# One batch of the samples' mLSTM states behind each tile of the output gate's projection

## The chip, the cores and the metric

The kernel runs on one core of a Trainium2 chip. Its time is the device time of one execution in microseconds (us); three runs of the kernel before gave 2279.9 to 2281.02, median 2280.3. One further execution was recorded by the hardware profiler: 2277.65 us, of which 2275.9 lie between its first and its last instruction.

## What is computed

One inference step of a hybrid decoder layer, for a prompt (1024 tokens) and for samples (8 batches of 4 tokens), with the same weights; the kernel holds both as 1056 columns. What matters here is the mixer: an S5 branch, an mLSTM branch with four heads of 256 by 256 state, and gates that are projections of the same normalized input. Cut to the parts that the change touches:

```
u, qk_raw, v, o, ig, fg, gate_s5, gate_m = split(h @ w_in)
y_s5 = gelu(S5(u)); y_s5 = y_s5 * sigmoid(y_s5 @ s5_w_glu)
hm, c_new, n_new, m_new = mlstm(q, k, v, log_i, log_f, c0, n0, m0)
hm = rmsnorm(hm) * g_mhead * sigmoid(o)
merged = sigmoid(gate_s5) * (y_s5 @ w_s5_up) + sigmoid(gate_m) * (hm @ w_m_up)
x = x + merged @ w_out
```

For the samples every batch and head has its own state c0 (256 by 256): the step reads it (q times c0 goes into the numerator), scales it by a decay, adds k times v, and writes it back. That is 8 batches of 4 states, 256 KB each, read and written once.

## The kernel before

The program is traced in Python (`run`, L1511) for five engines and their DMA queues. The context is opened with `schedule_with_timeline_sim=True` (L1577): at build time a planner with a simulated timeline puts the instructions of each queue in order. Of what it holds ready it takes what was traced earlier, so the order of the Python calls is a priority, not the order on the chip. After the build every queue runs strictly in its own order.

Around the change, `run` calls in this order (L1535 to L1543):

- `head_proj` and `head_scan` for heads 0 to 3: the prompt's mLSTM, in 8 chunks a head. The running state sits in a tile called mlA; its last value goes out by two stores on SP, L1222 (the matrix, 256 KB) and L1223 (one column of it, 1 KB).
- `samples()` is called before the last `head_scan`. It prepares the samples' operands and returns the function `states`.
- `states()` (L1293): first the new n (matmul L1303, DVE L1308, transposes L1311). Then `snum`, the PSUM tile of the samples' numerator, is opened by the matmul L1316, and the loop over 8 batches begins. A batch takes two tiles c from the pool "slots" (34 buffers, shared by nearly all large tiles); each is filled by two loads from SP (L1329, 256 KB each) and gets a small DVE copy (L1330). One DVE product (L1325) masks the batch's k. Then come the small matmuls of q with the states (L1334, into `snum`) and of k with v (L1340, PSUM tile skv), four DVE updates of c (L1342) and four stores from the ACT queue (L1343). After the loop `head_out` normalizes `snum` (DVE, ACT and POOL, L1146 to L1158), the transpose hT_smp and a DVE product (L1346) follow, and two stores on SP put the samples' columns into the scratch d_hm (L1349).
- `proj_tanh(..., "og")`: the output gate o, 8 tiles of 128 rows. A tile is one weight load on SP (wr_og, L100), its split into two halves, and 3 column chunks of 24 matmuls (mm_og, L109 to L111); a chunk leaves through DVE L614 and ACT L615 and is stored to the scratch d_to (L616).
- `s5_out_load` (L1357): four tiles yf of the S5 result come back from the scratch d_y (pool "r", two buffers), each goes through a gelu on ACT into y5f (L1365, L1366) and is split into y5h (ACT L92) and y5l (DVE L93).
- `s5_out` (L1372): the matmuls mm_glu on y5h and y5l, the small transposes cvT of `conv_out`, the matmuls mm_s5u, and `gated_heads`, which loads d_hm and d_to back.

The loads of `s5_out_load`, and those of L1390, L1405 and L1406, go through one helper. It ties the load behind the instruction that was traced just before it on the same engine, here SP; the planner may not put it ahead of that one:

```
    def pinned_load(self, dst, src):
        self.tc.keep_in_program_order(self.nc.sync.dma_start(dst, src))
...
    def s5_out_load(self):
...
        for mt in range(4):
            yf = self.pr.tile([P, RW], F32, tag="r", name=f"yf{mt}")[:, :1088].rearrange("p (t c) -> p t c", t=8)
            self.pinned_load(yf, self.d_y[mt * P:(mt + 1) * P])
```

Of the kernel before, what the change touches and what calls it, by code (L numbers as in the profile page):

```python
# [7 lines left out]
F32 = mybir.dt.float32  # L8
# [7 lines left out]
P = 128  # L16
# [5 lines left out]
XW = 1096  # L22
# [13 lines left out]
class Kernel:  # L36
# [562 lines left out]
            for s in range(8):  # L599
                nc.sync.dma_start(self.d_u[8 * mt:8 * mt + 8, s], ut[:, s])  # L600

    def proj_tanh(self, xn, rb, w, dst, name):

        nc = self.nc
        for m in range(KT):
            wt = self.weight(w[:, m * P:(m + 1) * P], f"{name}{m}")
            self.tanh_tile(xn, rb, wt, dst[m], f"{name}{m}")

    def tanh_tile(self, xn, rb, wt, dst, name):
        nc = self.nc  # L610
        for j, (o, n) in enumerate(CH):
            ps = self.unit(wt, xn, j, f"{name}_{j}")
            t = self.pt.tile([P, 384], F32, tag="sg", name=f"t_{name}_{j}")[:, :n]
            nc.vector.tensor_tensor(t, ps, rb[:, o:o + n], ALU.mult)  # L614
            nc.scalar.activation(t, t, AF.Tanh, scale=0.5)  # L615
            nc.scalar.dma_start(dst[:, o:o + n], t)  # L616
# [619 lines left out]
    def samples(self):  # L1236

        nc, v, a, pc = self.nc, self.nc.vector, self.a, self.pc
# [5 lines left out]
        x = self.px.tile([P, XW], F32, tag="s", name="smA")  # L1244
        rb, W, asb = x[:, 0:32], x[:, 32:64], x[:, 64:192].rearrange("p (h t) -> p h t", h=4)
# [23 lines left out]
        s = self.pv.tile([P, 512], F32, tag="aux", name="sS")[:, :32]  # L1269
# [23 lines left out]
        def states():  # L1293

            for h in range(4):
                v.tensor_copy(bm4[:, 8 * h:8 * h + 8], self.bmask)
            for h in range(4):
                for g in range(4):
                    if g != h:
                        v.memset(bm4[32 * g:32 * g + 32, 8 * h:8 * h + 8], 0.0)  # L1300
            ps = self.pv.tile([P, 512], F32, tag="aux", name="nn")[:, :64].rearrange("p (k h b) -> p k b h", k=2, h=4)
            for kk in range(2):
                nc.tensor.matmul(ps[:, kk].rearrange("p b h -> p h b"), kT[:, kk * P:(kk + 1) * P], bm4.rearrange("p (h b) -> p h b", h=4), start=True, stop=True)  # L1303
            dv = self.decb.rearrange("p (h c) -> p c h", h=4)[:, 8:16]
            for kk in range(2):
                n3 = nn[:, kk].rearrange("p (b h) -> p b h", h=4)
                v.tensor_tensor(n3, nz[:, :, kk, 0].rearrange("p (b h) -> p b h", h=4), dv, ALU.mult)
                v.tensor_tensor(n3, n3, ps[:, kk], ALU.add)  # L1308
            ps = self.pv.tile([P, 512], F32, tag="aux", name="nnT")[:32, :256]
            for kk in range(2):  # L1310
                nc.tensor.transpose(ps[:, kk * P:(kk + 1) * P], nn[:, kk], self.ident)  # L1311
            no = self.pt.tile([P, 384], F32, tag="h", name="no")[:32, :256]
            v.tensor_copy(no, ps)
            nc.sync.dma_start(self.outs[11][0].rearrange("b h k -> (b h) k"), no)
            num = self.pv.tile([P, 512], F32, tag="aux", name="snum")[:, :258]
            nc.tensor.matmul(num, Pb, self.vs, start=True, stop=False)  # L1316
            for b in range(8):
                bs = slice(4 * b, 4 * b + 4)
                qb = qm[b % 2]
                if b > 1:  # L1320
                    v.memset(qb[:, :, 4 * b - 8:4 * b - 4], 0.0)
                v.tensor_tensor(qb[:, :, bs].rearrange("p (h k) t -> p h k t", k=2), self.qs[:, :, bs].rearrange("p (h k) t -> p h k t", k=2),
                                asb[:, :, bs].unsqueeze(2).to_broadcast([P, 4, 2, 4]), ALU.mult)
                km = kms[b % 2]
                v.tensor_scalar(km, K[:96, :NP].bitcast(F32).rearrange("p (h x) -> p h x", h=4), self.bmask[:96, b:b + 1], None, op0=ALU.mult)  # L1325
                for hh in range(2):
                    ct = self.px.tile([P, XW], F32, tag="s", name=f"c0_{b}{hh}")[:, :1032].rearrange("p (h k x) -> p h k x", h=2, k=2)
                    for i in range(2):
                        nc.sync.dma_start(ct[:, i, :, 0:256], a["state_mlstm_c"][0, b, 2 * hh + i].rearrange("(k p) x -> p k x", p=P))  # L1329
                    v.tensor_copy(ct[:, :, :, 256:258], nz[:, 4 * b + 2 * hh:4 * b + 2 * hh + 2])  # L1330
                    for kk in range(2):
                        for i in range(2):
                            h = 2 * hh + i
                            nc.tensor.matmul(num[32 * h:32 * h + 32], qb[:, 2 * h + kk], ct[:, i, kk],  # L1334
                                             start=False, stop=b == 7 and kk == 1)
                    for i in range(2):
                        h = 2 * hh + i
                        kv = self.pv.tile([P, 512], F32, tag="aux", name=f"skv{b}_{h}").rearrange("p (k x) -> p k x", k=2)
                        for kk in range(2):
                            nc.tensor.matmul(kv[:, kk], km[:, h, kk * P:(kk + 1) * P], V[:96, 256 * h:256 * h + 256], start=True, stop=True)  # L1340
                        cc = ct[:, i, :, 0:256]
                        v.scalar_tensor_tensor(cc, cc, self.decb[:, 16 * h + 8 + b:16 * h + 9 + b], kv, op0=ALU.mult, op1=ALU.add)  # L1342
                        nc.scalar.dma_start(self.outs[10][0, b, h].rearrange("(k p) x -> p k x", p=P), cc)  # L1343
            ps, hT = self.head_out(num, em, P, "smp")()
            gm = self.gain["g_mhead"]
            v.tensor_tensor(hT.rearrange("p k (h t) -> p k h t", h=4), ps.rearrange("p k (h t) -> p k h t", h=4),  # L1346
                            gm.rearrange("p (h k) -> p k h", k=2).unsqueeze(3).to_broadcast([P, 2, 4, 32]), ALU.mult)
            for kk in range(2):
                nc.sync.dma_start(self.d_hm[kk::2, :, NP:NT].rearrange("h p t -> p h t"), hT[:, kk].rearrange("p (h t) -> p h t", h=4))  # L1349
# [161 lines left out]
    def run(self):  # L1511
        a, nc = self.a, self.nc
        w_in = a["w_in"][0]
        self.consts()
        self.d_xs = self.pd.tile([KT, P, NT], F32, name="d_xs")
        self.d_h = {q: self.pd.tile([16, P, NT], F32, name=f"d_{q}h") for q in ("f1", "f2")}
        F, st = self.first_pair(a["w1_gate"][0], a["w1_up"][0], "f1")
        xm, hook, sm = self.norm("g_mix", "n2")
        self.ffn(a["w1_gate"][0], a["w1_up"][0], a["w1_down"][0], F, st, "f1", hook, u0=1)
        self.scratch()  # L1520
        for m in range(KT):
            nc.sync.dma_start(self.d_x[m], self.x[m])
        self.dump("x1", self.x)
        rb = sm["rb"]
        self.mlstm_consts()
        self.s5_load()
        self.gates(xm, rb, w_in)
        self.proj_u(xm, rb, w_in)
        self.s5_prep()
        self.head_setup()  # L1530
        self.s5()
        self.proj_tanh(xm, rb, w_in[:, 4616:5640], self.d_t5, "gs")
        self.proj_tanh(xm, rb, w_in[:, 5640:6664], self.d_tm, "gm")
        self.scan_setup()
        for h in range(4):  # L1535
            qkv = self.head_proj(xm, sm, w_in, h)
            if h == 3:
                states = self.samples()
            self.head_scan(h, *qkv)
        states()  # L1540
        self.proj_tanh(xm, rb, w_in[:, 3584:4608], self.d_to, "og")
        self.s5_out_load()
        self.s5_out()  # L1543
        F, hook, st = self.norm_s("g_ffn2", "n3")
        self.join(hook)
        self.dump("x2", self.x)
        xp, hook, sp = self.norm("g_ple", "n4", "x")
        self.ffn(a["w2_gate"][0], a["w2_up"][0], a["w2_down"][0], F, st, "f2", hook, self.ple_in)
        self.dump("x3", self.x)
        self.ple(xp, sp, self.output())  # L1550
        self.dump("x4", self.x)
# [29 lines left out]
```

## Time and profile before

| | us |
|---|---|
| median of 3 runs (lowest, highest) | 2280.3 (2279.9, 2281.02) |
| the profiled execution, its own time | 2277.65 |
| its span, first to last instruction | 2275.9 |
| TensorE matmuls (PE) busy | 2234.4 (98%) |
| VectorE (DVE) busy | 1385.0 (61%) |
| ScalarE (ACT) busy | 823.4 (36%) |
| mean TensorE clock granted, as a share of full speed | 0.995 |

The profiled execution lies 2.65 us under the median of the runs. Durations below come from it alone. In the rows, PE is the matmul stream and PEld its weight loads; SPq, ACTq and DVEq stand for what a queue itself does (issuing a DMA, waiting), which does not count as busy. An idle time stands in square brackets with what ended it. Matmuls overlap their neighbours: a record of 0.34 us takes some 0.18 us of the stream, as the starts of the records show.

### The profile page before, as it was taken

Reading aid. Unit: us, or ns where it says so; the run is one execution under the profiler, and the core shown is the slowest. Engines: PE = TensorE matmul, PEld = TensorE weight load, DVE = VectorE, ACT = ScalarE, POOL = GpSimd, SP = SyncE. Lnnn points to the kernel's source line nnn. Section 1 sums busy time; section 2 is a strip of 40 time slices with the busy share of each in tenths; the row PEclk is TensorE's granted clock in tenths of the full one; section 3 lists DMA queues with packets and bytes.
Section 4 is the critical chain, followed back from the end, with each engine's and each line's share of the span. In section 5 each row is a group of like instructions: output and inputs, shape, how many; then the busy total and the mean of one; then the engine's idle time right before and its main releaser. Section 6 shows DMA issues by size and latency. Waiting matters only on the chain.

```text
span 2275.9 us, 39780 instructions
## 1 busy us (share of the span) xinstructions
PE 2234.4 (98%) x15711; PEld 2198.8 (97%) x15711; DVE 1385.0 (61%) x3189; ACT 823.4 (36%) x1560; POOL 514.8 (23%) x536
## 2 busy tenths in 40 slices
PE   7899999999999999999999999999999999999999
PEld 6899999999999999999999979999999999999998
DVE  5855556335868857678686477546655456523754
ACT  6433323113434433344444333224433233311543
POOL 1576664000000100000000000003476666100000
PEclk9999999999999999999999999999999999999999
DMA  6123226322454542112223587442222232711201
GB/s 198 59 76 94 71 61 232 123 72 69 125 125 125 142 127 67 52 48 69 64 58 97 162 277 249 136 149 83 64 71 81 75 95 86 269 64 54 61 20 77
DMA packets 288099, 240.47 MB, mean 106 GB/s; under 512 B 28652, under 2 KB 266188, under 8 KB 287912
## 3 DMA queue, kind: packets, MB, share of 16 engines
q1 hardware_dynamic: 268672, 216.34, 31.1%
q10 hardware_dynamic: 19240, 21.59, 2.8%
q8 instruction: 123, 2.02, 0.4%
q14 instruction: 64, 0.52, 0.1%
HBM read 168.04 MB, written 67.35 MB: 103 GB/s over the span
## 4 chain that ended last, share of the span: by engine, by line
PE 91%; DVE 5%; DMA 2%; issue 1%; ACT 1%; POOL 1%; SPq 1%; POOLq 0%; ACTq 0%; DVEq 0%
PE mm_qk L111 3%; PE mm_qk L110 3%; PE mm_qk L109 3%; PE mm_f1d L109 2%; PE mm_f1d L110 2%; PE mm_f1d L111 2%; PE mm_f2d L111 2%; PE mm_f2d L109 2%; PE mm_f2d L110 2%; PE mmc_f2u L185 2%; PE mma_f2u L185 2%; PE mmd_f2u L185 2%; PE mmc_f2g L185 2%; PE mmd_f2g L185 2%; PE mmd_f1g L185 2%; PE mmd_f1u L185 2%
## 5 line engine op out<-in xcount | busy, mean ns | idle before, releaser
L109 PE MATMUL mm_qk<-n2h,wh_qk 128*128 128x384 f32 (+1 forms) x384 | 125.7, 327 | 0.0
L110 PE MATMUL mm_qk<-n2l,wh_qk 128*128 128x384 f32 (+1 forms) x384 | 125.7, 327 | 0.0
L111 PE MATMUL mm_qk<-n2h,wl_qk 128*128 128x384 f32 (+1 forms) x384 | 125.5, 327 | 0.0
L109 PE MATMUL mm_f1d<-f1hh,wh_f1d 128*128 128x384 f32 (+1 forms) x384 | 122.9, 325 | 1.7 <-DVE x_f L551 1.7
L109 PE MATMUL mm_f2d<-f2hh,wh_f2d 128*128 128x384 f32 (+1 forms) x384 | 123.6, 326 | 0.5 <-DVE x_f L551 0.5
L111 PE MATMUL mm_f2d<-f2hh,wl_f2d 128*128 128x384 f32 (+1 forms) x384 | 124.0, 324 | 0.0
L110 PE MATMUL mm_f1d<-f1hl,wh_f1d 128*128 128x384 f32 (+1 forms) x384 | 123.9, 324 | 0.0
L111 PE MATMUL mm_f1d<-f1hh,wl_f1d 128*128 128x384 f32 (+1 forms) x384 | 123.6, 323 | 0.0
L110 PE MATMUL mm_f2d<-f2hl,wh_f2d 128*128 128x384 f32 (+1 forms) x384 | 123.5, 323 | 0.0
L1152 POOL TENSOR_TENSOR cy<-cs,mhalf 128x1 f32<-128x1 f32 x32 | 20.2, 631 | 443.9 <-DVE cs L1151 420.9
L415 POOL TENSOR_TENSOR rc_n<-nv_n,mhalf 128x3 f32<-128x3 f32 x9 | 8.8, 983 | 434.9 <-DVE nv_n L411 405.9
L551 DVE SCALAR_TENSOR_TENSOR x_f<-mm_f2d,x_f 128x384 f32<-128x384 f32 (+1 forms) x72 | 37.0, 518 | 93.6 <-PE mm_f2d L111 90.9
L551 DVE SCALAR_TENSOR_TENSOR x_f<-mm_f1d,x_f 128x384 f32<-128x384 f32 (+1 forms) x72 | 36.9, 520 | 93.6 <-PE mm_f1d L111 92.9
L1094 DVE SCALAR_TENSOR_TENSOR cv<-raw,vecs,cv 128x384 f32<-128x384 f32 (+1 forms) x144 | 84.7, 588 | 7.4 <-ACT cv L1092 6.1
L109 PEld LDWEIGHTS mm_f1d<-f1hh,wh_f1d 128*128 128x128 f32 x384 | 71.9, 188 | 2.5 <-DVE x_f L551 2.4
L109 PEld LDWEIGHTS mm_f2d<-f2hh,wh_f2d 128*128 128x128 f32 x384 | 71.9, 188 | 1.4 <-DVE x_f L551 1.2
L110 PEld LDWEIGHTS mm_qk<-n2l,wh_qk 128*128 128x128 f32 x384 | 72.3, 188 | 0.1
L111 PEld LDWEIGHTS mm_qk<-n2h,wl_qk 128*128 128x128 f32 x384 | 72.2, 188 | 0.1
L109 PEld LDWEIGHTS mm_qk<-n2h,wh_qk 128*128 128x128 f32 x384 | 72.2, 188 | 0.0
L110 PEld LDWEIGHTS mm_f2d<-f2hl,wh_f2d 128*128 128x128 f32 x384 | 72.2, 188 | 0.0
L110 PEld LDWEIGHTS mm_f1d<-f1hl,wh_f1d 128*128 128x128 f32 x384 | 72.1, 188 | 0.0
L111 PEld LDWEIGHTS mm_f2d<-f2hh,wl_f2d 128*128 128x128 f32 x384 | 72.0, 188 | 0.1
(759 smaller groups left out, 7390.9 us busy)
## 6 DMA issues: line engine op xcount, KB each, us to landing
d_f1h<-f1h SPq DMA_DIRECT2D x16, 528.0 KB
f1hl<-d_f1h SPq DMA_DIRECT2D x16, 528.0 KB
x_f<-d_xs SPq DMA_DIRECT2D x16, 528.0 KB
d_f2h<-f2h SPq DMA_DIRECT2D x16, 528.0 KB
f2hl<-d_f2h SPq DMA_DIRECT2D x16, 528.0 KB
wr_qk<-in_w_in_dram SPq DMA_DIRECT2D x16, 512.0 KB
c<-in_state_mlstm_c_dram SPq DMA_DIRECT2D x32, 256.0 KB
out_dram<-c ACTq DMA_DIRECT2D x32, 256.0 KB
```

Source lines behind the costliest of these rows:

```text
L109: mm(ps, wh, xh, start=start, stop=False)
L110: mm(ps, wh, xl, start=False, stop=False)
L111: mm(ps, wl, xh, start=False, stop=stop)
L185: nc.tensor.matmul(ps, w[:, wq, i], f[q][:, xq, cs], start=start and i == j == 0, stop=i == n - 1 and j == 2, skip_group_check=not start)
L415: nc.gpsimd.tensor_tensor(r, ms, self.mhalf[:, :nt], ALU.pow)
L551: v.scalar_tensor_tensor(xs, ps, 0.5, xs, op0=ALU.mult, op1=ALU.add)
L1094: v.scalar_tensor_tensor(acc, raw[:, o + i:o + i + wd], self.cw[:, i, T:T + 1], acc, op0=ALU.mult, op1=ALU.add)
L1152: nc.gpsimd.tensor_tensor(y, ss, self.mhalf[:n, 0:1], ALU.pow)
```

## The change

`states` becomes a generator. Ahead of the loop it requests the state tiles of batches 0 and 1, it stops at the head of each batch, and at a batch's end it requests the tiles of the batch two further on. `run` advances it up to batch 0, then once after each tile of the output gate; the eighth advance does batch 7, `head_out` and the stores into d_hm. `s5_out_load` is called after that, as before.

```diff
-    def proj_tanh(self, xn, rb, w, dst, name):
+    def proj_tanh(self, xn, rb, w, dst, name, then=lambda m: None):
...
             self.tanh_tile(xn, rb, wt, dst[m], f"{name}{m}")
+            then(m)
...
+            cts = {}
+
+            def load(b):
+                cts[b] = []
+                for hh in range(2):
+                    ct = self.px.tile([P, XW], F32, tag="s", name=f"c0_{b}{hh}")[:, :1032].rearrange("p (h k x) -> p h k x", h=2, k=2)
+                    for i in range(2):
+                        nc.sync.dma_start(ct[:, i, :, 0:256], a["state_mlstm_c"][0, b, 2 * hh + i].rearrange("(k p) x -> p k x", p=P))
+                    cts[b].append(ct)
+
+            load(0)
+            load(1)
             for b in range(8):
+                yield
...
                 for hh in range(2):
-                    ct = self.px.tile([P, XW], F32, tag="s", name=f"c0_{b}{hh}")[:, :1032].rearrange("p (h k x) -> p h k x", h=2, k=2)
-                    for i in range(2):
-                        nc.sync.dma_start(ct[:, i, :, 0:256], a["state_mlstm_c"][0, b, 2 * hh + i].rearrange("(k p) x -> p k x", p=P))
+                    ct = cts[b][hh]
...
+                if b < 6:
+                    load(b + 2)
...
-        states()
-        self.proj_tanh(xm, rb, w_in[:, 3584:4608], self.d_to, "og")
+        batches = states()
+        next(batches)
+        self.proj_tanh(xm, rb, w_in[:, 3584:4608], self.d_to, "og", lambda m: next(batches, None))
+        for _ in batches:
+            pass
```

## Rows read from the trace of the kernel before

**Rows 1.** The page: busy time of the engines over the span.
```profile
PE 2234.4 (98%) x15711; PEld 2198.8 (97%) x15711; DVE 1385.0 (61%) x3189; ACT 823.4 (36%) x1560; POOL 514.8 (23%) x536
```
**Rows 2.** PE's waits: who waited for whom, us in total, times, longest.
```profile
PE nnT L1311 <- DVE smA L1308: 3.9, 1, 3.9
```
**Rows 3.** Stretches: length, busy of PE, PEld, DVE, ACT, POOL; PEclk, DMA share.
```profile
1303.90:1307.80 3.90, 0.01 (x1) 0.04 (x2) 0.36 (x3) 0.00 (x0) 0.00 (x0) 0.76 0.18 29
1307.80:1312.20 4.40, 4.40 (x18) 2.15 (x18) 1.68 (x4) 0.44 (x1) 0.00 (x0) 0.50 0.50 149
1312.20:1314.00 1.80, 1.80 (x23) 0.98 (x24) 1.79 (x6) 0.00 (x0) 0.00 (x0) 0.84 0.57 175
1314.00:1355.40 41.40, 41.40 (x290) 32.90 (x287) 27.68 (x61) 15.22 (x20) 0.54 (x1) 1.00 0.92 306
1355.40:1371.00 15.60, 14.85 (x95) 14.43 (x95) 14.74 (x31) 7.79 (x19) 0.00 (x0) 1.00 0.65 196
```
**Rows 4.** PE groups by shape, 1200 to 1300 us, then 1300 to 1362.
```profile
L109 PE MATMUL mm_og<-n2h,wh_og 128*128 128x384 f32 x96 | 33.0, 344 | 0.0
L109 PE MATMUL mm_og<-n2h,wh_og 128*128 128x288 f32 x43 | 12.8, 298 | 0.0
...
L109 PE MATMUL mm_og<-n2h,wh_og 128*128 128x384 f32 x32 | 10.9, 341 | 0.0
```
**Rows 5.** SP's queue in order of time: start, us until the last issue, count.
```profile
1250.41 0.33 SPq L1355 DMA_DIRECT2D yf<-d_y  x1
1271.73 0.88 SPq L1329 DMA_DIRECT2D c<-in_state_mlstm_c_dram  x2
1285.84 4.01 SPq L1329 DMA_DIRECT2D c<-in_state_mlstm_c_dram  x8
1295.83 0.56 SPq L1223 DMA_DIRECT2D out_dram<-mlA  x1
1296.44 11.39 SPq L1329 DMA_DIRECT2D c<-in_state_mlstm_c_dram  x3
1337.96 0.34 SPq L1355 DMA_DIRECT2D yf<-d_y  x1
1366.38 0.92 SPq L1349 DMA_DIRECT2D d_hm<-mlC  x2
1369.08 0.33 SPq L1355 DMA_DIRECT2D g<-d_t  x1
```
**Rows 6.** The issues of the output gate's weights, first and last start.
```profile
L100 SPq DMA_DIRECT2D wr_og<-in_w_in_dram x8: 368/372/390, 1118.4 to 1228.0; - x8
```
**Rows 7.** DVE in order of time: start, us, what, idle before and its end.
```profile
1275.68 0.17 DVE L1330 COPY c<-smA 128x8 f32<-128x8 f32 x1
1307.38 0.17 DVE L1330 COPY c<-smA 128x8 f32<-128x8 f32 x1 [7.80 <-DMA c<-in_state_mlstm_c_dram]
1346.78 0.22 DVE L1146 TENSOR_SCALAR cd_smp<-snum,scol 128x1 f32<-128x1 f32 x1 [0.80 <-PE snum L1334]
1361.62 0.47 DVE L1158 TENSOR_SCALAR mlC<-snum,cy_smp 128x256 f32<-128x256 f32 x1
```
**Rows 8.** Tiles y5f and y5h: ns min/median/max, first and last start.
```profile
L1365 ACT ACTIVATE y5f<-yf x4: 2162/2195/2261, 1335.6 to 1351.9; 128x1024 f32<-128x1024 f32 x4
L1366 ACT ACTIVATE y5f<-yf x4: 238/240/243, 1337.7 to 1354.0; 128x32 f32<-128x32 f32 x4
L92 ACT ACTIVATE y5h<-y5f x12: 428/508/512, 1354.2 to 1360.2; 128x384 fp32r<-128x384 f32 x8, 128x288 fp32r<-128x288 f32 x4
L93 DVE TENSOR_TENSOR y5l<-y5f,y5h x12: 445/546/558, 1354.7 to 1364.9; 128x384 fp32r<-128x384 f32 x8, 128x288 fp32r<-128x288 f32 x4
```
**Rows 9.** PE in order of time, at the end of the output gate.
```profile
1355.10 0.29 PE L111 MATMUL mm_og<-n2h,wl_og 128*128 128x288 f32 x1
1355.23 0.40 PE L1340 MATMUL skv<-smV,sm 96*128 96x256 f32 x2
1355.47 0.70 PE L109 MATMUL mm_glu<-y5h,wh_glu 128*128 128x384 f32 x3
```
**Rows 10.** The chain that ended last: start, us that the piece held the chain.
```profile
1362.65 0.44 PE cvT L1230 x4
1363.61 0.18 PE mm_glu L110
```

## The prediction

> **What bounds the kernel now.** I read the busy times first: the matmul stream is busy for 98% of the span [rows 1], so a change pays only where PE stands still or runs at a lower clock, and costs wherever it makes PE stand still. Next I read PE's waits for the states' stretch. One counts: 3.9 us at the transposes of the new n [rows 2]. The stretches show it from 1303.9 to 1307.8, and behind it 4.40 us at a granted clock of 0.50 (1.2 of 2.4 GHz) and 1.80 us at 0.84. From 1314.0 to 1355.4 PE is busy all the time at full clock, although the DMA engines are 0.92 busy with states [rows 3]. The reason is in the groups: 139 of the 192 matmuls of L109 for the output gate (96 wide, 43 narrow) ran before 1300, 5.8 of the 8 tiles, although `states()` is traced ahead of them; the other 53, 32 of them wide, lie between the states' batches [rows 4]. The planner already uses the gate as filler: in the last head's scan, then between the batches.
>
> The queue of SP shows that requests ahead of time exist too: ten tiles' loads are issued or under way by 1296.4, before batch 0 computes, each as soon as a slot is free [rows 5].
>
> **What the change moves.** *Order of gate and batches.* The eight batches' work is unchanged: per batch four loads on SP, a mask, two small copies and four updates on DVE, four stores from ACT, the small matmuls. Only the priorities change: gate tile m now goes ahead of batch m and later. Tiles 0 to 5 are all but done when the states begin, so batches 0 to 5 stay ahead of nearly everything left, as before. Only batches 6 and 7 now rank behind tiles 6 and 7. The matmuls are the same and PE was full: 0 us on PE from this by itself. What it delays is the end of `snum`, 1346.8 before [rows 7]; PE's share of the gate that can pass is bounded by the gate's end at 1355.1 [rows 9], and I take 0 to 6 us for the delay (the batches' own PE and DVE work fills the rest).
>
> *Two batches of loads ahead.* Ten tiles were already ahead: nothing gained. Above, below: the 3.9 us stall. It comes from a copy L1330 of batch 4 that sits on DVE ahead of L1308 and waits 7.80 us for its load [rows 7]; that load was issued at 1296.44 behind the 1 KB column store of 1295.83, and the next one waited on SP for mlA's stores until 1306.9 [rows 5]. L1308 keeps its rank over every batch in both kernels, and batch 4's load has the same slot to wait for: I leave the stall where it is. If it went, the gain is 3.9 us, plus half of 4.40 us, plus 0.3 us of the 1.80 us at 0.84 (0.32 of it at half clock): 6.4 us.
>
> *What is traced last on SP before `s5_out_load`.* This is the term I take to decide. `pinned_load` ties yf0 to the SP instruction traced just before it. Before, that was the last weight load of the gate, issued at 1228.0 [rows 6], and yf0 was issued at 1250.41 [rows 5], 85 us before its gelu [rows 8]. The change traces batch 7, `head_out` and the d_hm stores L1349 after gate tile 7. So yf0 is now tied behind L1349, which before was issued at 1366.38 [rows 5]: behind the samples' whole head. Behind yf0 on SP stand yf1 to yf3 and, tied in turn, the loads of g, hm and to; for yf0 waits the gelu, for that the splits, and for those mm_glu, which is the only large PE work left when the gate is done.
>
> The sum, with T the issue of the first L1349:
> - T. Before, `head_out` took from 1346.8 to 1366.4, 19.6 us, for a chain whose own instructions need about 4 (my estimate: some ten DVE, ACT and POOL instructions of 0.15 to 0.5 us like L1146 and L1158 [rows 7]), because the planner put c updates and y5 splits between them. Without y5 work there is less to put between. Bounds 4 and 19.6, I take the middle, 12. T = 1347 + 12 = 1359; bounds 1351 and 1372 (1346.8 + 6 + 19.6).
> - From T to a complete first chunk of y5: 0.9 us for the two stores' issue and yf0's [rows 5]. Landing about 3.95 us, as the pair of loads of 1271.73 took to the copy at 1275.68 (512 KB against 544 [rows 5, 7]). A gelu is 2.20 + 0.24 = 2.44 us [rows 8], so gelu 0 ends at T + 7.3. The pool has two buffers: yf2 is issued only then and lands at T + 11.2, gelu 2 ends at T + 13.7; yf3 is issued when gelu 1 ends (T + 9.7), lands at T + 13.7, gelu 3 ends at T + 16.1. A split adds 0.51 + 0.55 [rows 8]: T + 17.2.
> - What PE has in the meantime. Gate and states end by about 1356.4 if PE stays full (five pairs of skv follow the gate's end, the first at 1355.23; 0.24 us of stream each between 1355.23 and 1355.47 [rows 9]). Then cvT, 4 by 0.44 = 1.8 us, and the part of mm_glu that needs only the first three y5 tiles: 4 PSUM banks (the pool of L49) by 9 matmuls by 0.18 [rows 10] = 6.3 us. Splits went after all four gelus before because the last gate matmul at 1355.1 freed the slots for y5h only then; now the slots are free first, so I let PE have these 6.3 us.
> - Loss: 1359 + 17.2 - 1356.4 - 1.8 - 6.3 = 11.7 us. Bounds: T = 1351 gives 3.7; T = 1366.4 (as before) with the 6.3 us not hidden gives 25.4.
> - Clock. Behind the 3.9 us stall PE lost 2.5 us at the lower clock [rows 3]; this idle time is longer, but the matmuls that follow it at first wait for gelus in any case. Bounds 0 and 2.5; I take 0.3.
>
> The Trainium skill, "TensorE: Matmul & The Clock Gate", section "HAM oscillation", says that matmuls after a long wait start cold and names that an extra loss beside the wait. Charged in full, the sum would be 14 us in place of 12; the trace agrees with the rule at 1307.8, and no row shows it for matmuls that trickle.
>
> Sum: +12.0 us. Against the profiled execution that is 2277.65 + 12.0 = 2289.65; the median of the runs is 2.65 higher, so I predict 2292.3.
>
> **The rivals.** *Hidden anyway (no change).* The tie costs nothing if T is so early that T + 17.2 lies before the end of gate and states plus 8.1 us of cover: T before 1347. That needs `snum` to be complete by 1343, 4 us earlier than now, against a lower rank; or the planner keeps yf0 in front, and the tie does not hold. For it: nothing in the rows; the order of SP (yf, then g) agrees with ties [rows 5]. Time 2280 (2276 to 2285).
>
> *Faster.* The stall at 1303.9 goes, since the planner places batch 4's copy behind L1308 now, and the tie is hidden: 2280.3 - 6.4 = 2273.9. The Trainium skill, "Perfetto Trace Analysis", section "Optimization Strategy", says that regimes bound by different engines gain from being interleaved; here the gate (PE) and the states (DMA). The rows speak against it: they are interleaved already [rows 3, 4], and the most that is left is the 6.4 us. With the tie in force as well, 2286.
>
> *Slower for another reason: the last batches' updates.* They fall into a stretch where DVE is busy for 14.74 of 15.60 us [rows 3]. Batches 6 and 7 have eight updates; pushed back by at most 6 us they would cost PE that much, if all of it is exposed: 2280 to 2286. It decides only where the tie does not.
>
> **How the numbers follow.** A measurement of this kernel can tell about 0.2%, 4.6 us, from no change. Chances: the tie as summed 0.72 (its own range 2284 to 2306); hidden 0.13; faster 0.08; the updates alone 0.07. The range leaves out part of the last three and the top: 2281 to 2304. Slower by over 0.2%: 0.70 of the tie, 0.04 of the updates and 0.01 of the hidden case, 0.75; within 0.2%: the rest of these, 0.02 + 0.03 + 0.12 = 0.17; faster: 0.08.
>
> **What would show it.** Right: on SP yf0 is issued behind L1349; PE idles some 10 us between the last skv and the full rate of mm_glu, in PE's waits put down to y5h or y5l, with a lower granted clock there; gelus between some 1360 and 1380; 1200 to 1300 us unchanged, and the 3.9 us at nnT still there. Wrong: yf0 is issued before L1349, or L1349 comes before 1350; then the time stays near 2280. If nnT's wait is gone, the sum is 6.4 us lower.

## The result, and the profile of the changed kernel

The change makes the kernel slower. The median of its runs is 2301.79 us (2300.8 to 2302.74), that of the kernel before in the same comparison 2280.1 us (2276.39 to 2281.02): a ratio of 1.0105, interval 1.0093 to 1.0117. The profiled execution took 2302.32 us with a span of 2300.6, so 24.7 us more than the one of before. The prediction had the direction and the place, and half of the size; the time lies near the upper end of its range, 2281 to 2304.

In the changed kernel the loop over the batches has lines 1330 to 1357, the samples' stores into d_hm are L1363 (L1349 before), the pinned loads L1369 (L1355), the gelus L1379 and L1380 (L1365 and L1366), L1146 has become L1147 and the transposes of the new n L1312.

The page's line of busy times, to be held against [rows 1]:

```profile
PE 2236.3 (97%) x15711; PEld 2199.8 (96%) x15711; DVE 1384.3 (60%) x3189; ACT 824.0 (36%) x1560; POOL 515.8 (22%) x536
```

The instructions are the same in number. PE's idle time (span less busy) went from 41.5 to 64.3 us, its busy time up by 1.9 us: 22.8 + 1.9 = 24.7. PE's waits in the changed kernel from 1300 to 1460 us (who waited for whom, us, times, longest; a fourth, of 0.3 us at skv, is left out):

```profile
PE mm_glu L109 <- ACT y5h L92: 14.6, 1, 14.6
PE nnT L1312 <- DVE smA L1309: 6.0, 1, 6.0
PE hT_smp L1164 <- DVE mlC L1159: 5.2, 1, 5.2
```

Before, the only waits of this stretch were the one of [rows 2] and this one, from the same view:

```profile
PE hT_smp L1163 <- DVE mlC L1158: 0.7, 1, 0.7
```

So one wait is new, the one for y5h; the one for the head (hT_smp) has grown from 0.7 to 5.2 us, and the one at nnT from 3.9 to 6.0. The stretches of the changed kernel, with the columns of [rows 3]:

```profile
1308.00:1314.00 6.00, 4.77 (x20) 2.44 (x24) 2.93 (x8) 0.44 (x1) 0.00 (x0) 0.53 0.42 140
1314.00:1355.50 41.50, 41.50 (x297) 33.48 (x289) 27.68 (x57) 3.60 (x6) 0.00 (x0) 0.99 0.82 269
1355.50:1360.20 4.70, 4.19 (x28) 2.21 (x27) 4.02 (x9) 1.39 (x2) 0.00 (x0) 1.00 0.65 216
1360.20:1365.00 4.80, 0.00 (x0) 0.00 (x0) 2.75 (x10) 1.85 (x3) 0.54 (x1) 0.79 0.98 330
1365.00:1369.00 4.00, 3.85 (x18) 2.99 (x18) 0.43 (x2) 0.00 (x0) 0.00 (x0) 0.50 0.24 43
1369.00:1383.30 14.30, 0.23 (x2) 0.00 (x0) 0.68 (x1) 8.58 (x9) 0.00 (x0) 0.62 0.49 161
1383.30:1387.50 4.20, 3.72 (x13) 3.72 (x14) 3.89 (x8) 4.20 (x12) 0.00 (x0) 0.57 0.81 274
```

Gate and states keep PE full up to 1355.5, and for 4.19 of the next 4.70 us. Then PE stands, does 3.85 us of transposes (hT_smp and cvT) at a granted clock of 0.50, stands again until 1383.78, and starts mm_glu in a stretch with a granted clock of 0.57. Before, mm_glu followed the gate's last matmul within half a microsecond [rows 9]. ACT's 15.22 us in the stretch to 1355.4 [rows 3] are 3.60 now: the gelus are gone from there. Where they are, the tiles say, with the columns of [rows 8], and with them the end of the gate and of `snum`:

```profile
L1379 ACT ACTIVATE y5f<-yf x4: 2013/2030/2031, 1372.2 to 1381.1; 128x1024 f32<-128x1024 f32 x4
...
L92 ACT ACTIVATE y5h<-y5f x12: 427/508/513, 1383.2 to 1387.5; 128x384 fp32r<-128x384 f32 x8, 128x288 fp32r<-128x288 f32 x4
...
L111 PE MATMUL mm_og<-n2h,wl_og x192: 290/336/527, 1211.5 to 1355.5; 128*128 128x384 f32 x128, 128*128 128x288 f32 x64
...
L1346 PE MATMUL snum<-c,smA x64: 378/382/642, 1313.7 to 1357.8; 128*32 128x258 f32 x64
```

And the reason why they are late stands in SP's queue in order of time, to be held against [rows 5]:

```profile
1366.31 1.75 SPq L1363 DMA_DIRECT2D d_hm<-mlC  x2
1368.10 8.64 SPq L1369 DMA_DIRECT2D yf<-d_y  x4
```

yf0, issued at 1250.41 before, is now issued at 1368.10, right behind the two d_hm stores. The chain that ended last passes through the same places (start, us that the piece held the chain):

```profile
1366.31 0.37 SPq L1363
...
1368.10 4.04 DMA yf<-d_y
1372.16 2.03 ACT y5f L1379
...
1376.43 4.69 DMA yf<-d_y
...
1383.32 0.42 ACT y5h L92
1383.78 1.65 PE mm_glu L109 x4
```

### The profile page after: what moved, and what is told of

Its sections match the earlier page's. It is cut to its first block, busy times and chain, and to the rows that moved or that the text cites. A ratio compares the mean times of both kernels' runs of the same rounds, so it can differ in the third digit from the quotient of the medians.

```text
span 2300.6 us, 39773 instructions
## 1 busy us (share of the span) xinstructions
PE 2236.3 (97%) x15711; PEld 2199.8 (96%) x15711; DVE 1384.3 (60%) x3189; ACT 824.0 (36%) x1560; POOL 515.8 (22%) x536
## 4 chain that ended last, share of the span: by engine, by line
PE 87%; DVE 5%; issue 4%; DMA 2%; ACT 1%; SPq 1%; POOL 1%; ACTq 0%; POOLq 0%; DVEq 0%
PE mm_qk L111 3%; PE mm_qk L110 3%; PE mm_qk L109 3%; PE mm_f2d L111 3%; PE mm_f2d L110 3%; PE mm_f2d L109 3%; PE mm_f1d L109 2%; PE mm_f1d L110 2%; PE mm_f1d L111 2%; PE mma_f2u L185 2%; PE mmd_f2u L185 2%; PE mmc_f2u L185 2%; PE mmc_f2g L185 2%; PE mmd_f2g L185 2%; PE mmd_f1g L185 2%
```

## The experiments

Three questions were open. Is it the tie alone, or also the order in which the batches compute? Why is the loss twice the sum? And what makes the wait at nnT, which both kernels have? "The kernel before" is measured again on the chip of each comparison, with medians from 2278.26 to 2278.93.

**The tie taken away, the interleaving kept** (`e1`): yf0 is tied to the last weight load of the gate, as before.

```diff
-        nc.sync.dma_start(raw, src.rearrange("(k p) m -> p k m", p=P))
+        self.last_w = nc.sync.dma_start(raw, src.rearrange("(k p) m -> p k m", p=P))
...
-            self.pinned_load(yf, self.d_y[mt * P:(mt + 1) * P])
+            if mt == 0:
+                with self.tc.issue_after(self.last_w.ins):
+                    self.nc.sync.dma_start(yf, self.d_y[:P])
+            else:
+                self.pinned_load(yf, self.d_y[mt * P:(mt + 1) * P])
```

> The changed kernel with one edit: the first yf load is tied behind the last weight load of the output gate, as it was before the change, instead of behind the samples' d_hm stores. Theory A (the tie makes the loss): the yf loads are issued before 1345 us again, PE's waits for y5h and for the samples' transposes go, and the time comes back to 2277 to 2285 us. Theory B (the batches between the gate's tiles make the loss, by their order on PE and DVE): the time stays above 2293 us and PE stands still for over 10 us although yf is early.

Measured: 2285.75 us, ratio 1.0036 (1.0023 to 1.0049). That is just above the range for the tie. Some 16 us of the loss are gone, and 7.5 us against the kernel before (2278.26) remain. PE's waits of this kernel from 1300 to 1460 us, then SP's queue in order of time:

```profile
PE nnT L1312 <- DVE smA L1309: 5.1, 1, 5.1
PE mm_s5u L109 <- DVE g L1412: 3.0, 3, 1.6
PE mm_mu L109 <- DVE g L1412: 2.7, 1, 2.7
PE mm_glu L110 <- DVE y5l L93: 1.3, 2, 1.1
```

```profile
1250.77 0.33 SPq L1379 DMA_DIRECT2D yf<-d_y  x1
...
1376.43 0.92 SPq L1363 DMA_DIRECT2D d_hm<-mlC  x2
...
1398.17 1.57 SPq L1369 DMA_DIRECT2D g<-d_t  x1
```

yf0 is early again and PE runs from the gate into mm_glu. But the samples' head, begun at 1357.69 instead of 1346.78 [rows 7], is now in DVE's queue among the splits and products of S5, and its stores come at 1376.43 instead of 1366.38 [rows 5]. The second load of g, tied behind hm and to, is issued at 1398.17, where it was issued at 1385.65 before, and PE waits 5.7 us for the products with g. This order of the traces has a price, which the prediction set at 0 on PE; `e7` below shows that it lies in the last batch alone.

**The tie alone, without the interleaving** (`e2`): the kernel before, with yf0 tied behind the d_hm stores.

```diff
-                nc.sync.dma_start(self.d_hm[kk::2, :, NP:NT].rearrange("h p t -> p h t"), hT[:, kk].rearrange("p (h t) -> p h t", h=4))
+                self.head_st = nc.sync.dma_start(self.d_hm[kk::2, :, NP:NT].rearrange("h p t -> p h t"), hT[:, kk].rearrange("p (h t) -> p h t", h=4))
...
+            if mt == 0:
+                with self.tc.issue_after(self.head_st.ins):
+                    self.nc.sync.dma_start(yf, self.d_y[:P])
+            else:
+                self.pinned_load(yf, self.d_y[mt * P:(mt + 1) * P])
```

> The kernel before with one edit: the first yf load is tied behind the samples' d_hm stores; states and gate keep their old order. Theory A: most of the loss comes without any interleaving; batches 6 and 7 are not held back by gate tile 7, so the head's stores are issued some 6 to 12 us earlier than in the changed kernel and the time is 2288 to 2296 us. Theory B: no loss, 2277 to 2285 us.

Measured: 2305.02 us, ratio 1.0113 (1.0096 to 1.013), 26.8 us over the kernel before: the whole loss, and more than was expected. PE's waits from 1300 to 1460 us, SP's queue, and DVE in order of time, where the head's first and last instructions stand:

```profile
PE mm_glu L109 <- ACT y5h L92: 17.8, 1, 17.8
PE nnT L1311 <- DVE smA L1308: 5.7, 1, 5.7
```

```profile
1365.61 1.40 SPq L1349 DMA_DIRECT2D d_hm<-mlC  x2
1367.06 1.71 SPq L1365 DMA_DIRECT2D yf<-d_y  x1
```

```profile
1351.22 0.22 DVE L1146 TENSOR_SCALAR cd_smp<-snum,scol 128x1 f32<-128x1 f32 x1 [1.88 <-PE snum L1334]
...
1361.26 2.71 DVE L1342 SCALAR_TENSOR_TENSOR c<-c,decb,skv 128x512 f32<-128x512 f32 x4
1363.89 1.22 DVE L93 TENSOR_TENSOR wl_s5u<-wr_s5u,wh_s5u 128x1024 fp32r<-128x1024 f32 x1
1365.02 0.42 DVE L1346 TENSOR_TENSOR mlC<-hT_smp,vecs 128x256 f32<-128x256 f32 x1
```

Here `snum` is ready 7 us earlier than in the changed kernel, and the stores come at about the same time, because DVE puts c updates and a weight split ahead of the head's last product. An early `snum` does not make an early head. The wait at nnT is 5.7 us here, without any interleaving, so its growth in the changed kernel (3.9 to 6.0) goes with the tie; with yf0 issued early it is 4.7 in `e7` and 5.1 in `e1`. The two prices do not add: 26.8 alone and 7.5 alone, and together 21.7 (the result) to 25.3 (a second comparison, below), which fits two delays on the one path from the head.

**The requests ahead alone** (`e3`): all batches are traced ahead of the gate, with loads two ahead.

```diff
-        self.proj_tanh(xm, rb, w_in[:, 3584:4608], self.d_to, "og", lambda m: next(batches, None))
         for _ in batches:
             pass
+        self.proj_tanh(xm, rb, w_in[:, 3584:4608], self.d_to, "og")
```

> The changed kernel with all eight batches traced ahead of the gate, as before, so that only the request of the states two batches ahead is left of the change. Both theories: no difference that can be measured, 2277 to 2284 us, ten tiles requested before batch 0 as before. If the requests ahead themselves did harm (slots taken early), it would be over 2285 us.

Measured: 2278.82 us, ratio 1.0001 (0.9991 to 1.001). Worth nothing, as worked out.

**One batch earlier** (`e7`): the generator is advanced once more ahead of the gate. Batch 7, `head_out` and the d_hm stores are then traced behind tile 6, and the last instruction on SP ahead of yf0 is the weight load of tile 7.

```diff
         next(batches)
+        next(batches)
         self.proj_tanh(xm, rb, w_in[:, 3584:4608], self.d_to, "og", lambda m: next(batches, None))
```

> The changed kernel with one more advance ahead of the gate: batch m+1 behind gate tile m, so batch 7, the samples' head and its d_hm stores are traced ahead of gate tile 7, and the last instruction traced on SP ahead of the yf loads is a weight load of the gate again. Theory A: the first yf load is issued before 1345 us, the 24 us go, and with the head no longer behind gate tile 7 the 7 us that were left with the tie undone shrink too: 2277 to 2284 us. If interleaving as such costs what was left with the tie undone, it is 2284 to 2289 us.

Measured: 2278.3 us, ratio 0.9997 (0.9988 to 1.0006). SP's queue and DVE in order of time:

```profile
1250.41 0.33 SPq L1369 DMA_DIRECT2D yf<-d_y  x1
...
1366.54 0.92 SPq L1363 DMA_DIRECT2D d_hm<-mlC  x2
```

```profile
1346.92 0.22 DVE L1147 TENSOR_SCALAR cd_smp<-snum,scol 128x1 f32<-128x1 f32 x1 [0.79 <-PE snum L1346]
```

yf0, the end of `snum` and the d_hm stores are back within 0.2 us of the kernel before [rows 5, 7]. One line takes the whole loss away, so the loss is made of what the eighth advance puts behind the last tile (the tie and the late head together), and the interleaving of the other batches costs nothing that can be measured and brings nothing.

**The cover** (`e4`, and `e10` in five rounds): the prediction let PE have 6.3 us of mm_glu between the gelus. In the changed kernel ACT ran all gelus first. Here each gelu is followed by the split of its first chunk; the other chunks stay in their loop.

```diff
             self.y5f.append(y)
-        for o, n in CH:
+            self.split(y[:, :384], *(t[:, :384] for t in self.y5[mt]))
+        for o, n in CH[1:]:
```

> The changed kernel with one edit: the first chunk of each y5 tile is split right behind the tile's gelu, instead of behind all four gelus. The prediction let PE do 6.3 us of mm_glu while the later gelus run, and the changed kernel shows none of it. If the order of the splits on ACT is why, the first mm_glu starts some 7 us earlier and the time falls by 4 to 6.3 us, to 2295 to 2298 us. If something else holds mm_glu, it stays at 2301 to 2303 us.

Measured: 2302.34 us (2297.94 to 2304.17), ratio 1.0102 (1.0086 to 1.0117), too wide to tell a few us. So once more, with the changed kernel itself beside it on the same chip:

> The kernel of e4 once more, beside the changed kernel on the same chip, since four runs of it spread over 6 us. In its profile mm_glu began 11 us earlier than in the changed kernel and PE waited 8 us less for y5h. If that work counts (the prediction's 6.3 us of cover), it is 4 to 6 us under the changed kernel; if the later chunks hold the stage back anyway, it is within 2 us of it.

> The changed kernel as it is, for the comparison with e10 on the same chip: 2300 to 2304 us by every theory.

Measured: 2302.44 us (ratio 1.0102, 1.0085 to 1.0118) against 2303.57 us of the changed kernel (1.0107, 1.0092 to 1.0122); the kernel before had 2278.28. The medians are 1.1 us apart, with intervals that overlap. The split tile in `e10`, PE's waits, and one stretch:

```profile
L92 ACT ACTIVATE y5h<-y5f x12: 427/507/528, 1374.7 to 1385.7; 128x384 fp32r<-128x384 f32 x8, 128x288 fp32r<-128x288 f32 x4
```

```profile
PE mm_glu L109 <- ACT y5h L92: 7.6, 3, 6.3
...
PE mm_glu L109 <- ACT glt L1396: 2.9, 1, 2.9
```

```profile
1365.00:1383.00 18.00, 11.41 (x47) 9.85 (x48) 4.65 (x10) 10.34 (x16) 0.00 (x0) 0.69 0.44 132
```

PE did get the work: it begins mm_glu at 1375.3 and is busy for 11.41 us of the stretch to 1383 (4.08 in the changed kernel). But part of that ran at a lower clock (0.69 in the mean of the stretch), and then PE waits again, for the last tile's split and for glt. Its last mm_glu starts at 1406.0 instead of 1408.2. Two traces of each kernel can be compared. From the first d_hm store to the start of the last mm_glu the changed kernel takes 41.9 us and, in `e11`, 42.1; with the split earlier it is 39.9 in `e10` and 37.9 in `e4`, whose profiled execution was its fastest by 4 us. The cover is worth 2 to 4 us in the traces, not 6.3, and no more than about 1 us in the medians, which is not clear of noise.

**The wait at nnT** (`e5`, `e6`, on the kernel before). The prediction put it down to a copy L1330 that stands ahead of L1308 on DVE and waits for a load. `e6` takes the copies behind the new n; `e5` takes away what the load may be waiting for, the last head's 1 KB column store, by copying the column to a small tile and storing it behind the states.

```diff
-                v.tensor_tensor(n3, n3, ps[:, kk], ALU.add)
+                nnop = v.tensor_tensor(n3, n3, ps[:, kk], ALU.add)
...
-                    v.tensor_copy(ct[:, :, :, 256:258], nz[:, 4 * b + 2 * hh:4 * b + 2 * hh + 2])
+                    with self.tc.issue_after(nnop.ins):
+                        v.tensor_copy(ct[:, :, :, 256:258], nz[:, 4 * b + 2 * hh:4 * b + 2 * hh + 2])
```

> The kernel before with the batches' small copies on DVE planned behind the new n's DVE operation; the column store stays where it is. If the order on DVE is what makes PE wait, nnT's wait goes (under 0.5 us) and the time falls by 3 to 6.4 us, to 2272 to 2277 us. If the transfers hold the batches anyway, a wait of the same length appears at the first batches instead (at snum or skv) and the time stays within 2 us of before.

Measured: 2279.84 us, ratio 1.0003 (0.9994 to 1.0012). PE's waits, and DVE in order of time:

```profile
PE skv L1341 <- DVE no L1313: 4.0, 1, 4.0
```

```profile
1312.41 0.17 DVE L1331 COPY c<-smA 128x8 f32<-128x8 f32 x1 [8.32 <-DMA c<-in_state_mlstm_c_dram]
1312.49 0.41 DVE L1313 COPY no<-nnT 32x256 f32<-32x256 f32 x1
```

The wait only moved one step on: a copy that waits for its load now holds the next DVE instruction that PE needs. The order on DVE is where it shows, not where it comes from.

```diff
-        nc.sync.dma_start(self.outs[5][0, 0, h].rearrange("(k p) -> p k", p=P), Cp[:, :, 256])
+        if h < 3:
+            nc.sync.dma_start(self.outs[5][0, 0, h].rearrange("(k p) -> p k", p=P), Cp[:, :, 256])
+        else:
+            self.ncol = self.pc.tile([P, 2], F32, name="ncol")
+            v.tensor_copy(self.ncol, Cp[:, :, 256])
...
         states()
+        self.pinned_load(self.outs[5][0, 0, 3].rearrange("(k p) -> p k", p=P), self.ncol)
```

> The kernel before with the 1 KB column store of the last head's state taken out of the way: the column is copied to a small tile and stored behind the samples' d_hm stores. If the column store's slow landing is what holds batch 4's load, the copy on DVE and so the new n (3.9 us of idle time on PE and 2.5 us at the lower clock), PE's wait at nnT falls under 1.5 us and the time by 4 to 6.4 us, to 2272 to 2276 us. If the wait comes from the many loads queued ahead instead, it stays near 3.9 us and the time within 2 us of before.

Measured: 2275.47 us, ratio 0.9986 (0.9977 to 0.9995). Two of the stretches of [rows 3] in this kernel:

```profile
1303.90:1307.80 3.90, 3.90 (x28) 2.86 (x27) 1.75 (x4) 1.50 (x2) 0.00 (x0) 1.00 0.48 153
1307.80:1312.20 4.40, 4.40 (x42) 3.32 (x41) 2.63 (x8) 0.00 (x0) 0.00 (x0) 1.00 0.85 273
```

The wait and the low clock are both gone, for 3 us of the 6.4 us that the prediction gave for it. Where the rest went stands in the trace. By the starts of the matmuls, the way from the gate's first to the first mm_glu takes 138.4 us (1212.6 to 1351.0) against 144.8 before (1210.7 to 1355.5): the whole 6.4 us. Up to the first mm_mu only 3.9 are left. The column is now stored at 1362.91, just ahead of the loads of g, hm and to, and SP waits longer there for the stores of cvo, which hold a buffer that a load needs. SP's queue, this wait from 1360 to 1400 us, and the same wait before:

```profile
1362.91 0.60 SPq L1359 DMA_DIRECT2D out_dram<-ncol  x1
```

```profile
SPq L1359 <- DMA out_dram<-cvo: 12.7, 4, 10.7
```

```profile
SPq L1355 <- DMA out_dram<-cvo: 5.1, 2, 4.4
```

So the edit moved part of the store's price behind mm_glu; what a store without this price would give was not run.

**Put together** (`e8`, `e9`): the edits of `e7` and `e5`, on the changed kernel, and those of `e5` and `e6`, on the kernel before. Of the first pair, one line of each edit:

```diff
+            self.pinned_load(self.outs[5][0, 0, 3].rearrange("(k p) -> p k", p=P), self.ncol)
...
         next(batches)
+        next(batches)
```

> Both mendings on the changed kernel: one batch more traced ahead of the gate, and the last head's column copied and stored behind the d_hm stores. The two act on different stalls (the tie at 1366 us, the wait at nnT near 1304 us), so the gain over the kernel before should be that of the column alone, 3 us: 2274 to 2277 us. If interleaving has a worth that the tie hid, it is under 2273 us; if they hinder each other, over 2278 us.

> The kernel before with the column store late and the batches' copies planned behind the new n. With the column out of the way batch 4's load lands early, so the order on DVE has nothing left to cost: 2274 to 2277 us, as with the late column alone. If the two waits were separate, it would be 2270 to 2273 us.

Measured: 2275.52 us, ratio 0.9985 (0.9976 to 0.9994), and 2275.48 us, 0.9988 (0.998 to 0.9997), against 2278.93. Both are what the column alone gives. So the version that beats both kernels is the kernel before with the late column; with that stall gone too, the interleaving still brings nothing.

## Why the prediction was right in kind and short by half

**Right: the tie decides, and where.** yf0 behind the d_hm stores, gelus from 1372 to 1381, PE's wait put down to y5h, a lower clock there, nnT's wait still there: all as listed. `e1` (the tie alone taken away) and `e2` (the tie alone put in) show it. From T, the first d_hm store, to the complete first chunk the prediction worked out 17.2 us; mm_glu began after 17.5 (1366.31 to 1383.78). That is in part luck: the last gelu ended 17.0 us after T and not 16.1, and PE began behind the first tile's y5h, 0.4 us later, not behind a whole split of 1.1.

**Right: loads ahead are worth nothing** (`e3`), and there was little to gain by interleaving (`e7`, `e8`). Not ten but nine tiles had their loads issued by 1296.4, the ninth's second one last; the tenth's were issued from 1306.94. The rival that rests on the Trainium skill's "Perfetto Trace Analysis", section "Optimization Strategy", which says that interleaving regimes may improve performance, is not borne out here (ratio 0.9997 in `e7`): the regimes were interleaved already.

**Wrong: three terms of the sum**, all in the same direction (the delay of `snum` inside T, the cover, the clock), and two that made up for a part (the head's own chain and the end of the states):

| term | predicted | profile after |
|---|---|---|
| T, first d_hm store | 1359 | 1366.31 |
| T to the first mm_glu | 17.2 | 17.5 |
| end of gate and states on PE | 1356.4 | 1360.2 |
| PE's work from there to mm_glu | 1.8 + 6.3 = 8.1 | 3.85 + 0.23 = 4.1 |
| PE stands still | 11.7 | 1383.8 - 1360.2 - 4.1 = 19.5 |
| clock | 0.3 | 3.2 |

With the 2.1 us that nnT's wait grew, and less the 0.7 us for hT_smp of before, the right column gives 24.1 of the 24.7 us. The match of the parts is looser: these terms make 20.9 us of idle time where the page has 22.8, and 3.2 us of slower work where its busy time rose by 1.9.

- *T: "I take 0 to 6 us for the delay"* of `snum`, of which the sum (T = 1347 + 12) used 0. It was 11.8: L1146 at 1346.78 [rows 7] against, on DVE in order of time,

```profile
1358.55 0.21 DVE L1147 TENSOR_SCALAR cd_smp<-snum,scol 128x1 f32<-128x1 f32 x1
```

  The last `snum` matmul starts at 1357.8, behind the gate's last at 1355.5. Batch 7 is traced behind the whole of tile 7, and its matmuls came behind it. The prediction knew that rank and named the gate's end as a bound, which alone gives 8.3 us (1346.8 to 1355.1), and then counted nothing. The head's own chain (taken as 12, between 4 and 19.6) was shorter, 7.8 us, since DVE had less else to do, as argued. T lay inside its bounds, 1351 and 1372; the second error took back a part of the first.
- *"so I let PE have these 6.3 us"*. ACT ran all four gelus first, as before; free slots for y5h did not change that. And by `e10` the term was too large even with the work given: PE starts 8.5 us earlier and ends only 2 us earlier (4 in the trace of `e4`). A reading that fits, argued and not shown: the first chunk ends with the last tile, so work that is brought forward shortens only what is left behind that tile.
- *Clock: 0.3*. In the changed kernel 3.85 us were done at 0.50 and 3.72 us at 0.57, which loses 1.9 + 1.6 us by the prediction's reckoning (time times the missing share of the clock); the states' stretch lost 2.2 (4.77 us at 0.53) against 2.5. That is 3.2 us more. The matmuls that trickle were slow too. By the rule of the Trainium skill's "TensorE: Matmul & The Clock Gate", section "HAM oscillation", the sum would have been 14 by the prediction's own reckoning. The trace agrees with that rule here: the loss stands beside the wait.
- *"0 us on PE from this by itself"* for the order of gate and batches. In `e1` it is 7.5 us, 5.7 of them in waits for the products with g: the late head holds the loads of g, hm and to. In the changed kernel it is hidden under the tie. The prediction had seen these loads behind yf0, but not that they wait for the head in any case.

The upper bound that the prediction gave, T as before and no cover, was 25.4 us: nearly what happened. The sum took a middle for the head, 0 for the delay and the full cover where the reasons for the bounds (a rank behind the gate; gelus traced ahead of the splits) held.

**Half right: nnT.** The copy on DVE was named as the cause, and the column store as what its load was issued behind. `e6` and `e5` show that the store counts and the copy's place does not. The 6.4 us for the end of the wait are there in the trace of `e5` up to mm_glu; 3 are left in the medians, as the moved store delays what follows it.

## What to carry to other kernels

Where a helper ties an instruction to "the one traced just before", moving a piece of the trace moves the tie: list what is last on each queue at the place of the move, before and after. Put what a tie will be hung on ahead of the last filler, not behind it; here one batch earlier was the difference between +22 to +25 us and nothing. And when the rank of a delayed piece is known, take the delay that the rank gives (behind all of the filler), not the low end of a range.

## What the runs showed of the hardware

In this kernel a 1 KB store holds up far larger transfers. Before the change, these are SP's longest wait from 1295 to 1310 us, and the chain of waits at the same place:

```profile
SPq L1329 <- DMA out_dram<-mlA: 9.7, 1, 9.7
```

```profile
1295.83 11.04 DMA out_dram<-mlA
...
1306.94 0.37 SPq L1329
```

The column, 256 elements of 4 bytes each from its own place, was issued at 1295.83 [rows 5], and 11.04 us went by until it had landed. Two things waited. The load of batch 4 that was issued right behind it, at 1296.44, is the one that DVE's copy at 1307.38 waits for [rows 7], and with it nnT: 10.9 us, where the pair of loads of 1271.73 took 3.95 [rows 5, 7]. The next load takes mlA's own slot and stood at the head of SP's queue for 9.7 us. The matrix alone, stored from the same tile, does not do that: in `e5`, where only the column is read out to a small tile, the wait of the loads for mlA's store is 3.2 us, in the same view from 1290 to 1312 us:

```profile
SPq L1333 <- DMA out_dram<-mlA: 3.2, 1, 3.2
```

The traces also hold the times at which each transfer's semaphore counts were complete, and by these the store is slow everywhere: 8.8, 8.7, 8.9 and 11.0 us from issue to landing for the four heads of the kernel before, and 9.2 us in `e5` at its later place. Its neighbours wait with it: all six transfers that SP and ACT issued from 1294.88 to 1300.17, the column among them and the others of 128 to 256 KB, landed only between 1306.2 and 1307.9. In `e5` the matrix took 4.7 us, the load behind it 4.8, and at the store's new place the load of g issued at 1364.58 took 11.1 us, where it took 3.8 before.

The Trainium skill, "DMA: Bandwidth & Descriptors", section "Rules for kernel authors", says that a strided last dimension lowers to one descriptor per element and should be made contiguous. A store of 1 KB that takes this long fits that; a contiguous column was not tried.
